# Two more Strassen pairs in the output projections of a transformer block, and a later place for one load

## The chip, the cores and the metric

One core of a Trainium2 chip runs the whole program. The metric is the device time of one execution in microseconds; lower is better.

## The reference

One block of a streaming encoder on 256 tokens of width 2048, in float32: a SwiGLU feed-forward layer, a mixer of two attentions (A: 16 heads of 64 with a clipped relative bias; B: latent attention, 16 heads), cross attention over 256 memory tokens (4 heads of 512), and a second feed-forward layer, each with a residual and a layer norm behind it. What matters here is the output side of the mixer and of the cross attention:

```python
y_b = mla_attention(...) @ w_o_b                 # 256x2048 @ 2048x2048
mix = (g_a * y_a + g_b * y_b) @ w_out
h = layer_norm(ALPHA * h + mix, ...)
m = layer_norm(mem, mem_ln_g, mem_ln_b)          # 256 memory tokens
kv = m @ w_xkv ; q = h @ w_xq
xa = softmax(q @ k.T / sqrt(512)) @ v @ w_xo     # 256x2048 @ 2048x2048
h = layer_norm(ALPHA * h + xa, ...)
```

## The kernel before

**Arithmetic.** Each float32 operand is split into a high part `hi` (a cast to fp32r on ScalarE, L264) and a rest `lo` (a subtraction on VectorE, L267). A product is three TensorE passes: hi·hi, lo(x)·hi(w), hi(x)·lo(w).

**Units.** A weight matrix comes in raw tiles of 128x2048 (1 MB) through SyncE's DMA queue into three buffers, in the order of use, up to two units ahead of TensorE. In a *pair group* (`pair_group`) a unit holds two K tiles of 128 rows for 1024 columns of output. Group g makes 1024 of the 2048 columns for all 256 tokens, so a unit updates four PSUM tiles of 128x512; a 2048-row matrix has eight units, c = 0 to 7.

**Plain and Strassen units.** A plain unit (`mm_pair`, L311) is 2 K tiles x 4 PSUM tiles x 3 passes = 24 matmuls of 512 columns. A unit that is listed in the group's `at` is taken as one 2x2 Strassen-Winograd step (`mm_sums`, L366): seven products, 21 matmuls. It needs four sums of the weight's quarters (`weight_sums`, L248 and L250, VectorE), `hi` and `lo` of three of the raw quarters and of the four sums, and four sums of the activation (`sum_forms`, L321 and L325, then a split, L255 and L256). The order of its products is: high part of raw quarters, low part of them, high part of the sums, low part of the sums. When the next unit is a Strassen unit too, the halves change places, so that the buffers of the sums come free early (`close`). Behind the group's last Strassen unit `shared` combines four extra PSUM tiles (L679 to L684).

**Homes.** The host stores a Strassen unit's weight quarters in another order, so `at` is also an argument of the layout. `sums_in` names the blocks of on-chip memory for hi, lo and the staging of the sums; a `SUMS_` table names for each unit c the block in which the activation's sums stay, or `None` for small pool buffers.

**The order of work.** The kernel's Python code lists items; `weave` puts side work in front of the i-th item of a group. A tile framework then schedules all instructions, so an engine's order follows the list only roughly. On the chip each engine takes its instructions in its own fixed order.

**The places that are touched.**
- `out_b(g)` in `mixer`: the two groups of `y_b @ w_o_b`. Group 0 has Strassen units 2, 4, 6 (`AT_YB[0]`), group 1 has 4 and 6. Behind each group `done` multiplies by the gates (L1282 to L1284) and copies 16-bit planes (L846) for DMA transposes (L850), which SyncE issues between weight loads; `turn` joins the planes again (L854) and splits them (L255, L256) into the operand `mix` of the next product, 512 columns at a time. Group 0's transposes run during group 1, and group 1's during the first units of `mix @ w_out`.
- `mem_norm`: loads the memory tokens (`mem`, into blocks T1 and T2) and the transposed memory (`memT`, into T3 and H4) from GpSimd's DMA queue at item 0 of the `w_out` product. Statistics follow at items 4 and 7, and the quarters of the normalised memory at items 10 to 14.
- `cross`: the first output group of `w_xo` (`out_pair` with `SUMS_XO`) has Strassen units 2, 4, 6 in natural order. Among its first units stand the last two heads' products, `out(2)` and `out(3)` (L1543), which use the same kind of PSUM tile (`mm`) as the group's four extra tiles.

Of the kernel before, what the change touches and what calls it, by code (L numbers as in the profile page):

```python
# [21 lines left out]
KT = D // P  # L22
# [10 lines left out]
ORDER_GATE = (0, 2, 1, 4, 5, 3, 6, 7)  # L33
SUMS_YB = {4: ("T0", 0), 6: ("T0", 1), 2: None}
AT_YB = (2, 4, 6), (4, 6)
SUMS_XQ = {4: ("H5", 0), 6: ("H5", 1), 2: None}
SUMS_XV = {4: ("T3", 0), 6: ("T3", 1), 2: None}
SUMS_XO = {2: None, 4: ("H2", 0), 6: ("H2", 1)}

AT_XQ = (4, 6), (2, 4, 6)  # L40
AT_XV = (2, 4, 6), (4, 6)
SUM_HOME = ("X2", "X3"),
# [59 lines left out]
class Kernel:  # L102
# [515 lines left out]

    def out_pair(self, bank, src, g, nk, x, at, fx, scale, st, sums_in=SUM_HOME):

        nc, h = self.nc, self.h
        ps, qs = {}, {}
# [10 lines left out]
        def finish():  # L633
            for tt in range(2):
                for a in range(2):
                    self.finish(tt, 2 * g + a, ps[tt, a], scale and not at, st)
        self.pair_group(bank, src, 512, nk, x, at, fx, ps, qs, shared, sums_in)
        self.add(finish)
# [692 lines left out]
    def mem_norm(self):  # L1331

        nc, t = self.nc, self.t
        e = self.mem = {}

        def load():
            e["m"] = [self.block(f"T{1 + tt}", (P, D)) for tt in range(2)]
            e["raw"] = [self.block(g) for g in ("T3", "H4")]
            for j in range(2):
                nc.gpsimd.dma_start(e["m"][j], t["mem"][j])  # L1340
            for j in range(2):
                nc.gpsimd.dma_start(e["raw"][j], t["memT"][:, 8 * j:8 * j + 8, :])
# [40 lines left out]

        return {0: [load], 4: [stat(0)], 7: [stat(1)], 9: [spread], 10: [quarter(0)], 11: [quarter(1)], 13: [quarter(2)], 14: [quarter(3)]}

# [47 lines left out]
    def cross(self, xT, st, norm, steps_out):  # L1433
        nc, t, e = self.nc, self.t, self.mem
        q, k, v, sc, pt, o, turned = {}, {}, {}, {}, {}, {}, {}
        fq, fv, fx = {}, {}, {}
        m, x = lambda: e["mT"], lambda: o["t"]
# [113 lines left out]
        form = lambda c: self.forms_step(fx, SUMS_XO, c, x)  # L1551
# [14 lines left out]
        scale, planes, nsend, njoin = norm  # L1566
# [13 lines left out]
        def all_items():  # L1580
            self.out_pair(1, t["w_xo"][0], 0, KT, x, SUMS_XO, fx, True, st, (("T0", "T1"), "T3"))
            self.out_proj("w_xo_r", KT, x, True, st, steps_out, (
                ("T0", "T1", "early"), ("T2", "T3", "early"), ("H0", "H1", "early"), ("H2", "H3", "early")), 2)
        self.weave(self.collect(all_items), {1: [out(2), out(3), form(2)], 2: [form(4)], 4: [form(6)]}, prio=0)

# [191 lines left out]
```

## Time and profile before

| | |
|---|---|
| timed runs | 2434.51, 2434.72, 2436.06 us; median 2434.72 us |
| the profiled execution's own time | 2432.88 us |
| its span | 2431.0 us |
| granted TensorE clock | 1.000 |
| ScalarE, GpSimd busy | 1553.1 us (64%), 36.0 us (1%) |
| HBM traffic | 200 GB/s over the span |

Matmuls are pipelined and their ends are modelled, so a TensorE busy for 100% is told apart from a waiting one only by the start times of successive matmuls. Stretches in what follows are us from the span's start: `out_b(0)` runs from 1200.14 to 1241.62, `out_b(1)` to 1283.78, the first group of `w_out` to 1327.59, and the first output group of the cross attention, with the two heads' products in it, from 1649.68 to 1697.34.

### The profile page before, as it was taken

The page shows a single profiled execution, that of the slowest core. Times are in us where ns is not written, and L with a number is a line of the kernel's source. Part 1 is how long each engine was busy: PE and PEld are TensorE (multiplying, and loading weights), DVE is VectorE, ACT ScalarE, POOL GpSimd, SP SyncE. Part 2 cuts the span into 40 slices and gives each one's busy share as a digit, 9 for nine tenths or more (in the row PEclk, how much of TensorE's full clock was granted, in tenths as well). Part 3 has the DMA queues.
Part 4 walks back from the last instruction along what each step waited for, and adds up shares of the span by engine and source line. Part 5 has one row for each costly group of instructions (what it writes and reads, how often), then busy time and mean ns, then how long its engine had stood idle before and what let it go on. Part 6 is the DMA issues. An engine that isn't in the chain of part 4 may idle for free.

```text
span 2431.0 us, 29704 instructions
## 1 busy us (share of the span) xinstructions
PE 2422.4 (100%) x11280; PEld 2021.5 (83%) x11280; DVE 2131.3 (88%) x2437; ACT 1553.1 (64%) x2022; POOL 36.0 (1%) x81
## 2 busy tenths in 40 slices
PE   9999999999999999999999999999999999999999
PEld 8888888889888888888888888888888888888887
DVE  8999989899889998789788889879879999888997
ACT  6676745666555557878565787755666675556662
POOL 0000000000000001000000000000000000000000
PEclk9999999999999999999999999999999999999999
DMA  7766656667645657776577577655556766666665
GB/s 267 253 211 215 206 201 223 210 202 230 218 174 211 216 202 242 236 203 176 186 254 246 170 237 214 216 183 192 191 199 213 228 222 211 219 207 207 201 222 180
DMA packets 176416, 516.21 MB, mean 212 GB/s; under 512 B 111729, under 2 KB 112497, under 8 KB 121105
## 3 DMA queue, kind: packets, MB, share of 16 engines
q1 hardware_dynamic: 170816, 495.83, 61.5%
q0 software_dynamic: 4592, 17.30, 2.3%
q8 instruction: 88, 1.44, 0.2%
q10 hardware_dynamic: 864, 1.18, 0.1%
q14 instruction: 56, 0.45, 0.1%
HBM read 485.30 MB, written 2.10 MB: 200 GB/s over the span
## 4 chain that ended last, share of the span: by engine, by line
PE 89%; DVE 4%; ACT 3%; DMA 2%; issue 1%; SPq 0%; DVEq 0%; ACTq 0%
PE at L311 25%; PE mm L311 24%; PE at L366 11%; PE mm L366 11%; PE mm L298 10%; PE mm L277 4%; PE mm L279 2%; DVE lo L267 2%; ACT hi L264 2%; PE at L1034 1%; DMA raw<-w_xq 1%; DMA raw<-w_xk 0%; DMA raw<-w_xv 0%; PE at L1088 0%; ACT w L832 0%
## 5 line engine op out<-in xcount | busy, mean ns | idle before, releaser
L264 ACT CAST hi<-raw 128x1024 fp32r<-128x1024 f32 (+1 forms) x852 | 803.4, 980 | 440.4 <-PE at L311 130.5
L267 DVE TENSOR_TENSOR lo<-raw,hi 128x2048 fp32r<-128x2048 f32 (+1 forms) x427 | 902.2, 2115 | 136.1 <-ACT hi L264 129.1
L311 PE MATMUL mm<-hi,T 128*128 128x512 f32 (+1 forms) x1312 | 308.1, 384 | 0.5 <-ACT hi L255 0.4
L264 ACT CAST X<-H 128x1024 fp32r<-128x1024 f32 (+1 forms) x170 | 174.7, 1034 | 171.5 <-DVE H L248 117.5
L311 PEld LDWEIGHTS mm<-hi,T 128*128 128x128 f32 x1312 | 244.4, 188 | 46.8 <-ACT hi L255 0.9
L311 PE MATMUL at<-hi,T 128*128 128x512 f32 x1136 | 272.3, 390 | 0.0
L311 PEld LDWEIGHTS at<-hi,T 128*128 128x128 f32 x1136 | 213.3, 188 | 44.4
L267 DVE TENSOR_TENSOR X<-H,X 128x2048 fp32r<-128x2048 f32 (+1 forms) x85 | 191.5, 2253 | 62.1 <-ACT X L264 61.9
L311 PE MATMUL mm<-lo,T 128*128 128x512 f32 (+1 forms) x656 | 158.1, 383 | 0.0
L311 PE MATMUL at<-lo,T 128*128 128x512 f32 x568 | 141.0, 390 | 0.0
L311 PEld LDWEIGHTS mm<-lo,T 128*128 128x128 f32 x656 | 122.2, 188 | 22.4
L311 PE MATMUL at<-hi,H 128*128 128x512 f32 x560 | 133.4, 390 | 0.0
L311 PEld LDWEIGHTS at<-lo,T 128*128 128x128 f32 x568 | 106.7, 188 | 22.1
L311 PEld LDWEIGHTS at<-hi,H 128*128 128x128 f32 x560 | 105.0, 188 | 21.5
L250 DVE TENSOR_TENSOR H<-H,raw 128x512 f32<-128x512 f32 (+1 forms) x170 | 115.7, 681 | 2.4
L311 PE MATMUL mm<-hi,H 128*128 128x512 f32 x480 | 115.6, 392 | 0.4 <-DVE w L684 0.4
L311 PEld LDWEIGHTS mm<-hi,H 128*128 128x128 f32 x480 | 89.6, 188 | 19.5 <-DVE w L684 0.8
L248 DVE TENSOR_TENSOR H<-raw 128x1024 f32<-128x1024 f32 (+1 forms) x85 | 102.2, 1203 | 0.5 <-DMA raw<-w_gate 0.3
L366 PE MATMUL mm<-X,X 128*128 128x512 f32 x342 | 91.3, 392 | 0.0
L264 ACT CAST X<-raw 128x1024 fp32r<-128x1024 f32 (+1 forms) x54 | 55.4, 1035 | 48.7 <-DVE raw L250 38.7
L366 PE MATMUL at<-X,X 128*128 128x512 f32 (+1 forms) x315 | 82.7, 386 | 0.0
L854 ACT COPY w<-w 128x1024 uint16<-128x1024 uint16 (+1 forms) x60 | 75.6, 1273 | 1.5 <-DMA w<-w 1.4
(387 smaller groups left out, 4153.9 us busy)
## 6 DMA issues: line engine op xcount, KB each, us to landing
raw<-ffn_w_in SPq DMA_DIRECT2D x150, 1024.0 KB, 4.9
raw<-ffn_w_out SPq DMA_DIRECT2D x66, 1024.0 KB, 4.9
raw<-w_gate SPq DMA_DIRECT2D x32, 1024.0 KB, 4.7
raw<-ffn_w_out_r SPq DMA_DIRECT2D x16, 1024.0 KB, 5.0
raw<-w_qk SPq DMA_DIRECT2D x16, 1024.0 KB, 5.3
raw<-w_o_b SPq DMA_DIRECT2D x16, 1024.0 KB, 4.8
raw<-w_out SPq DMA_DIRECT2D x16, 1024.0 KB, 5.1
raw<-w_xk SPq DMA_DIRECT2D x16, 1024.0 KB, 5.3
```

Of the source, the lines that this page charges most:

```text
L248: self.nc.vector.tensor_tensor(two[0], two[1], raw[:, :m].unsqueeze(1).to_broadcast([P, 2, m]), ALU.add)
L250: self.nc.vector.tensor_tensor(t[:, a * m:a * m + m], t[:, b * m:b * m + m], raw[:, a * m:a * m + m], ALU.add)
L264: self.last_hi = self.nc.scalar.copy(hi[:, c:d], src[:, c:d])
L267: self.last_lo = self.nc.vector.tensor_tensor(lo[:, :n], src, hi[:, :n].bitcast(F32), ALU.subtract)
L277: self.nc.tensor.matmul(ps, hi[j], x.both(kt), start=(j == 0), stop=False)
L279: self.last_mm = self.nc.tensor.matmul(ps[:, :S], lo[j], x.at(0, kt), start=False, stop=(j == n - 1))
L298: self.last_mm = self.nc.tensor.matmul(ps, x.at(xi, kt)[:, tt * P:(tt + 1) * P], w[wi][:, j * 512 + c:j * 512 + c + m], start=(start and j ...
L311: self.last_mm = self.nc.tensor.matmul(ps[tt, g][:, :n], x.at(xi, kt)[:, tt * P:(tt + 1) * P], w[wi][:, c:c + n], start=first and j + wi + ...
L366: self.last_mm = self.nc.tensor.matmul(bank[:, :m], a[xi], v[wi][:, c * m:(c + 1) * m], start=own and first and wi + xi == 0, stop=own and ...
L854: self.nc.scalar.copy(self.words(u, n).rearrange("p (c k) -> p k c", k=2), self.words(s, n).rearrange("p (k c) -> p k c", k=2))
L1034: nc.tensor.matmul(ps[:, c0:c0 + nk], q[:, tt * P:(tt + 1) * P], k[:, :nk], start=(j == 0), stop=(j == len(parts) - 1))
```

## The change

It has three parts. **(1)** `out_b(1)` takes units 2, 4 and 6 as Strassen units instead of 4 and 6; the activation's sums for unit 2, which group 0 uses already, move from pool buffers to block F, so that they last through both groups. **(2)** The first output group of `w_xo` takes units 0, 2, 4 and 6 as Strassen units, and its units run in the order 1, 0, 3, 2, 4, 5, 6, 7; the sums for unit 0 are formed in front of the group's first item and live in block F. **(3)** In `mem_norm` the two loads of the transposed memory move from item 0 to item 5.

```diff
-SUMS_YB = {4: ("T0", 0), 6: ("T0", 1), 2: None}
-AT_YB = (2, 4, 6), (4, 6)
+SUMS_YB = {4: ("T0", 0), 6: ("T0", 1), 2: ("F", 0)}
+AT_YB = (2, 4, 6), (2, 4, 6)
-SUMS_XO = {2: None, 4: ("H2", 0), 6: ("H2", 1)}
+SUMS_XO, ORDER_XO = {2: None, 4: ("H2", 0), 6: ("H2", 1), 0: ("F", 0)}, (1, 0, 3, 2, 4, 5, 6, 7)
...
-    def out_pair(self, bank, src, g, nk, x, at, fx, scale, st, sums_in=SUM_HOME):
+    def out_pair(self, bank, src, g, nk, x, at, fx, scale, st, sums_in=SUM_HOME, order=None):
...
-        self.pair_group(bank, src, 512, nk, x, at, fx, ps, qs, shared, sums_in)
+        self.pair_group(bank, src, 512, nk, x, at, fx, ps, qs, shared, sums_in, order)
...
         def load():
             e["m"] = [self.block(f"T{1 + tt}", (P, D)) for tt in range(2)]
-            e["raw"] = [self.block(g) for g in ("T3", "H4")]
             for j in range(2):
                 nc.gpsimd.dma_start(e["m"][j], t["mem"][j])
+
+        def load_turned():
+            e["raw"] = [self.block(g) for g in ("T3", "H4")]
             for j in range(2):
                 nc.gpsimd.dma_start(e["raw"][j], t["memT"][:, 8 * j:8 * j + 8, :])
...
-        return {0: [load], 4: [stat(0)], 7: [stat(1)], 9: [spread], 10: [quarter(0)], 11: [quarter(1)], 13: [quarter(2)], 14: [quarter(3)]}
+        return {0: [load], 4: [stat(0)], 5: [load_turned], 7: [stat(1)], 9: [spread], 10: [quarter(0)], 11: [quarter(1)], 13: [quarter(2)], 14: [quarter(3)]}
...
-            self.out_pair(1, t["w_xo"][0], 0, KT, x, SUMS_XO, fx, True, st, (("T0", "T1"), "T3"))
+            self.out_pair(1, t["w_xo"][0], 0, KT, x, SUMS_XO, fx, True, st, (("T0", "T1"), "T3"), ORDER_XO)
...
-        self.weave(self.collect(all_items), {1: [out(2), out(3), form(2)], 2: [form(4)], 4: [form(6)]}, prio=0)
+        self.weave(self.collect(all_items), {0: [form(0)], 1: [out(2), out(3), form(2)], 2: [form(4)], 4: [form(6)]}, prio=0)
```

The scheduled order changes with it. ScalarE at the start of `out_b(1)`, before; H0 and H1 are the gate blocks of group 0 whose planes go to the transposes (L846), and the `raw` tiles 1574, 1581, 1584, 1587 are units 1, 2, 3, 4:

```order
L264 CAST hi_1575_9961<-raw_1574_9959 128x1024 x2
L264 CAST hi_1582_10010<-raw_1581_10008 128x1024
L846 COPY H0_885_5874<-H0_885_5874 128x1024 x2
L264 CAST hi_1582_10010<-raw_1581_10008 128x1024
L264 CAST hi_1585_10041<-raw_1584_10039 128x1024 x2
L846 COPY H1_933_6171<-H1_933_6171 128x1024 x2
L264 CAST hi_1589_10078<-raw_1587_10046 128x1024
L264 CAST hi_1589_10078<-raw_1587_10046 128x512
```

The same place after the change; raw 1571, 1574, 1584, 1587 are units 1, 2, 3, 4, X3 holds the weight sums of unit 2 and H5 their high part:

```order
L264 CAST hi_1572_9952<-raw_1571_9950 128x1024 x2
L264 CAST H5_1582_10010<-X3_1575_9959 128x1024
L264 CAST hi_1580_10005<-raw_1574_9957 128x1024
L846 COPY H0_885_5874<-H0_885_5874 128x1024 x2
L264 CAST hi_1580_10005<-raw_1574_9957 128x512
L264 CAST hi_1585_10041<-raw_1584_10039 128x1024
L846 COPY H1_933_6171<-H1_933_6171 128x1024 x2
L264 CAST H5_1582_10010<-X3_1575_9959 128x1024
L264 CAST hi_1585_10041<-raw_1584_10039 128x1024
L264 CAST hi_1593_10079<-raw_1587_10046 128x1024
```

Unit 2's raw quarters are cast in two instructions (1024 and 512 columns), its sums in two more. The second cast of the sums (the second H5 row) stands behind the two plane copies of H1.

ScalarE in the first output group of the cross attention, before; X2 and X3 become the operands of the output product for heads 2 and 3, T3 and T0 hold a Strassen unit's weight sums and their high part, here those of unit 2, and w1 the activation's sums for it:

```order
L255 CAST X2_2065_13374<-mm_2067_13384 128x256
L255 CAST X2_2065_13374<-mm_2068_13393 128x256
L264 CAST T0_2063_13369<-T3_2054_13318 128x1024
L255 CAST X2_2065_13374<-mm_2069_13402 128x256
L264 CAST T0_2063_13369<-T3_2054_13318 128x1024
L255 CAST X3_2070_13411<-mm_2071_13412 128x256
L255 CAST X3_2070_13411<-mm_2072_13421 128x256
L255 CAST X3_2070_13411<-mm_2073_13430 128x256
L255 CAST X3_2070_13411<-mm_2074_13439 128x256
L264 CAST hi_2082_13493<-raw_2081_13491 128x1024 x2
L255 CAST w1_2075_13448<-w2_2080_13453 128x128
```

And after; T3 and T0 belong to unit 0 here, and F holds its activation's sums:

```order
L255 CAST X2_2070_13387<-mm_2072_13397 128x256
L255 CAST X2_2070_13387<-mm_2073_13406 128x256
L255 CAST X2_2070_13387<-mm_2074_13415 128x256
L264 CAST T0_2054_13317<-T3_2047_13271 128x1024
L255 CAST F_2058_13336<-w2_2060_13338 128x512
L255 CAST X3_2075_13424<-mm_2076_13425 128x256
L255 CAST X3_2075_13424<-mm_2077_13434 128x256
L255 CAST X3_2075_13424<-mm_2078_13443 128x256
L255 CAST X3_2075_13424<-mm_2079_13452 128x256
L264 CAST hi_2090_13505<-raw_2068_13381 128x1024
L255 CAST w1_2080_13461<-w2_2085_13466 128x128
```

The cast into F, one row behind unit 0's second T0 cast, now stands in front of the four casts of head 3 (X3).

TensorE at the same place, before; H4 and H5 are the operands for heads 0 and 1, hi_2051 and lo_2052 the plain unit 1, and the products of head 3 write mm tiles from X1 and X0:

```order
L311 MATMUL at_2057_13336<-hi_2051_13311,H4_1973_12758 128x512 x2
L1543 MATMUL mm_2071_13412<-X1_2039_13209,X0_2056_13329 128x256 x6
L311 MATMUL at_2058_13337<-hi_2051_13311,H4_1973_12758 128x512 x2
L1543 MATMUL mm_2072_13421<-X1_2039_13209,X0_2056_13329 128x256 x6
L1543 MATMUL mm_2073_13430<-X1_2039_13209,X0_2056_13329 128x256 x6
L1543 MATMUL mm_2074_13439<-X1_2039_13209,X0_2056_13329 128x256 x6
L311 MATMUL at_2059_13338<-hi_2051_13311,H4_1973_12758 128x512 x2
L311 MATMUL at_2060_13339<-hi_2051_13311,H4_1973_12758 128x512 x2
L311 MATMUL at_2057_13336<-lo_2052_13312,H4_1973_12758 128x512
```

And after; T0 and T1 are the high and low part of unit 0's weight sums, hi_2066 and lo_2067 the plain unit 3, and hi_2052 raw quarters of unit 0:

```order
L366 MATMUL at_2063_13348<-T0_2054_13317,H4_1973_12755 128x512 x2
L311 MATMUL at_2061_13346<-hi_2066_13376,H5_2000_12936 128x512 x2
L311 MATMUL at_2064_13349<-hi_2066_13376,H5_2000_12936 128x512 x2
L311 MATMUL at_2061_13346<-lo_2067_13377,H5_2000_12936 128x512
L311 MATMUL at_2064_13349<-lo_2067_13377,H5_2000_12936 128x512
L311 MATMUL at_2061_13346<-lo_2067_13377,H5_2000_12936 128x512
L311 MATMUL at_2064_13349<-lo_2067_13377,H5_2000_12936 128x512
L366 MATMUL at_2063_13348<-T1_2055_13318,H4_1973_12755 128x512
L311 MATMUL at_2063_13348<-hi_2066_13376,H5_2000_12936 128x512 x4
L311 MATMUL at_2063_13348<-lo_2067_13377,H5_2000_12936 128x512 x2
L366 MATMUL at_2062_13347<-hi_2052_13312,F_2058_13336 128x512
L1545 MATMUL mm_2076_13425<-X1_2039_13206,X0_2057_13329 128x256 x6
```

Head 3's products now stand behind the first product with T1 and the first with F.

GpSimd's queue with the memory loads, before; the row ahead of them clears a constant tile that `stat(0)` uses:

```order
L1349 MEMSET w1_1643_10438 128x128
L1340 DMA T2_1622_10291<-mem 128x2048
L1342 DMA T3_1623_10292<-memT 128x2048
L1342 DMA H4_1624_10293<-memT 128x2048
L1340 DMA T1_1621_10290<-mem 128x2048
```

And after:

```order
L1351 MEMSET w1_1641_10431 128x128
L1339 DMA T2_1622_10288<-mem 128x2048
L1344 DMA T3_1651_10486<-memT 128x2048
L1344 DMA H4_1652_10487<-memT 128x2048
L1339 DMA T1_1621_10287<-mem 128x2048
```

The four loads stand in the same order behind the same row: `mem` into T2, `memT` into T3 and H4, `mem` into T1.

## The prediction

> **What bounds the kernel now.** The page's first part and its summary of the chain of waits come first.
>
> ```profile
> PE 2422.4 (100%) x11280; PEld 2021.5 (83%) x11280; DVE 2131.3 (88%) x2437; ACT 1553.1 (64%) x2022; POOL 36.0 (1%) x81
> PE 89%; DVE 4%; ACT 3%; DMA 2%; issue 1%; SPq 0%; DVEq 0%; ACTq 0%
> ```
>
> TensorE (PE) is the bound, and VectorE (DVE) is close behind at 88%. How close it is in the touched places is read from the windows, one for each output group: length, then busy time and count of instructions by engine. The first two are untouched groups of the feed-forward layer for comparison, with four Strassen units each; then come `out_b(1)`, the first group of `w_out`, and the output group of the cross attention.
>
> ```profile
> core 0: us, PE busy (x) PEld busy (x) DVE busy (x) ACT busy (x) POOL busy (x), PEclk, DMA share, GB/s
> 729.03:769.83 40.80, 40.80 (x181) 33.81 (x181) 35.86 (x30) 23.24 (x28) 0.00 (x0) 1.00 0.63 222
> 769.83:811.49 41.66, 41.63 (x181) 33.58 (x181) 38.30 (x30) 25.06 (x28) 0.53 (x1) 1.00 0.57 198
> 1241.62:1283.78 42.16, 42.16 (x188) 34.93 (x186) 38.28 (x35) 30.44 (x35) 1.60 (x3) 1.00 0.82 276
> 1283.78:1327.59 43.81, 43.81 (x194) 35.97 (x193) 34.63 (x43) 26.78 (x29) 0.53 (x1) 1.00 0.79 252
> 1649.68:1697.34 47.66, 47.66 (x233) 39.87 (x232) 47.16 (x64) 28.78 (x43) 0.00 (x0) 1.00 0.54 186
> ```
>
> The clock is 1.00 throughout. VectorE fills 38.28 of 42.16 us in `out_b(1)` (91%) and 47.16 of 47.66 us (99%) in the cross output group: there it is as much the bound as TensorE.
>
> The price of a matmul comes from the timeline of TensorE, from start to start.
>
> ```profile
> 1649.68 3.79 PE L311 MATMUL at<-hi,H 128*128 128x512 f32 x16
> 1653.31 1.98 PE L311 MATMUL at<-lo,H 128*128 128x512 f32 x8
> 1655.12 3.04 PE L1543 MATMUL mm<-X,T 128*128 128x256 f32 x24
> 1657.99 2.46 PE L311 MATMUL at<-hi,H 128*128 128x512 f32 x10
> ```
>
> A plain unit, 24 matmuls, takes 1655.12 - 1649.68 = 5.44 us, or 0.2267 us each, and the next starts with no gap. A Strassen unit's 21 take 4.76 us. A head's 24 narrow products take 2.87 us.
>
> **What the two pairs remove and add.** Each pair removes three matmuls: 2 x 3 x 0.2267 = **1.36 us** on TensorE. What a Strassen unit asks of VectorE is seen just there, in the rows of unit 2.
>
> ```profile
> 1653.63 2.29 DVE L267 TENSOR_TENSOR lo<-raw,hi 128x2048 fp32r<-128x2048 f32 x1
> ...
> 1656.44 1.23 DVE L248 TENSOR_TENSOR T<-raw 128x1024 f32<-128x1024 f32 x1
> 1657.57 1.76 DVE L267 TENSOR_TENSOR lo<-raw,hi 128x1536 fp32r<-128x1536 f32 x1
> 1659.24 0.69 DVE L250 TENSOR_TENSOR T<-T,raw 128x512 f32<-128x512 f32 x1
> ...
> 1660.17 0.69 DVE L250 TENSOR_TENSOR T<-T,raw 128x512 f32<-128x512 f32 x1
> ...
> 1661.98 2.29 DVE L267 TENSOR_TENSOR T<-T,T 128x2048 fp32r<-128x2048 f32 x1
> ```
>
> A plain unit needs the first row alone, 2.29. A Strassen unit needs 1.23 + 2 x 0.69 for the weight's sums, 1.76 for the raw quarters' low part and 2.29 for the sums': 6.66, that is **4.37 us more**. The cross output also forms the activation's sums for unit 0.
>
> ```profile
> 1672.27 0.70 DVE L321 TENSOR_TENSOR w<-X 128x512 f32<-128x512 f32 x1
> 1673.00 0.50 DVE L325 TENSOR_TENSOR w<-w 128x128 f32<-128x128 f32 x2
> 1673.41 0.29 DVE L325 TENSOR_TENSOR w<-w,w 128x128 f32<-128x128 f32 x1
> ...
> 1675.69 0.28 DVE L325 TENSOR_TENSOR w<-w,w 128x128 f32<-128x128 f32 x1
> 1675.92 2.29 DVE L267 TENSOR_TENSOR T<-T,T 128x2048 fp32r<-128x2048 f32 x1
> 1678.12 0.68 DVE L256 TENSOR_TENSOR H<-w,H 128x512 fp32r<-128x512 f32 x1
> ```
>
> That is 0.70 + 0.50 + 0.29 + 0.28 + 0.68 = 2.45, so 6.8 us of VectorE go into the cross output group, and 4.4 into `out_b(1)`, where the activation's sums exist already. ScalarE gets some 1.5 us of casts a unit. SyncE's weight loads stay: a stored unit has the same bytes.
>
> **Term 1, `out_b(1)`.** These are the rows of TensorE (units 2, 3, 4 and 5 start at 1252.50, 1257.94, 1263.38 and 1268.14), of VectorE and of ScalarE.
>
> ```profile
> 1252.50 3.79 PE L311 MATMUL at<-hi,T 128*128 128x512 f32 x16
> 1257.94 3.79 PE L311 MATMUL at<-hi,T 128*128 128x512 f32 x16
> 1263.38 0.61 PE L366 MATMUL at<-hi,H 128*128 128x512 f32 x2
> 1268.14 3.79 PE L311 MATMUL at<-hi,H 128*128 128x512 f32 x16
> 1251.58 1.22 DVE L1284 TENSOR_TENSOR H<-H 128x1024 f32<-128x1024 f32 x1
> 1264.44 1.23 DVE L248 TENSOR_TENSOR X<-raw 128x1024 f32<-128x1024 f32 x1 [2.27 <-DMA raw<-w_o_b]
> 1252.84 2.00 ACT L846 COPY H<-H 128x1024 uint16<-128x1024 uint16 x2
> 1261.93 2.00 ACT L264 CAST hi<-raw 128x1024 fp32r<-128x1024 f32 x2 [2.09 <-DMA raw<-w_o_b]
> 1263.84 2.58 ACT L854 COPY H<-H 128x1024 uint16<-128x1024 uint16 x2
> ```
>
> An engine takes its rows in order, so the new order decides. (a) The second cast of unit 2's sums stands behind the two H1 copies, which wait for L1284, ready at about 1251.9: copies to 1253.9, cast (half of 2.00) to 1254.9, VectorE's low part (2.29, and a hand-over) to 1257.3. TensorE asks for that part after 17 of 21 matmuls, at 1252.50 + 3.85 = 1256.35: a wait of **1.0**. (b) The same cast of unit 4 stands behind both casts of unit 5's weights, which land at 1261.93, and behind one L854 copy: 1261.9 + 1.9 + 1.3 + 1.05 + 2.3 = 1268.5, half a microsecond more if the load comes as late as (a) makes it, say 1268.75. Unit 4 starts at 1263.38 - 0.68 + 1.0 = 1263.7 and asks at 1267.55: a wait of **1.2**. (c) For unit 6 the casts of unit 7 stand in front, whose buffer comes free some 3.8 us into unit 5: 3.8 + 1.9 + 2.2 + 2.3 = 10.2, against 5.44 + 3.85 = 9.3: **0.9**. So 3.1 of waits less 0.68 saved, **+2.4**. If nothing stood badly, VectorE's 42.16 - 38.28 = 3.9 idle and its lead would hide the 4.4, and the term is -0.7; if the casts come twice as late as needed, 6.2 - 0.7 = +5.5.
>
> I take +2.4: no row before shows a ScalarE instruction passing another that stands ahead of it.
>
> The Trainium skill, "TensorE: Matmul & The Clock Gate", section "Architectural detail: the array is 16× 32×32, not 1× 128×128", says that only TensorE may take a weight load ahead of its turn and that ScalarE and VectorE work strictly in order. By it this term would be +2.4; if a ready cast could pass a waiting copy it would be -0.7. The rows of before agree with it.
>
> **Term 2, the first group of `w_out`.** VectorE comes out of `out_b(1)` later by up to 4.4 - 2.4 = 2.0 us against TensorE, and group 1's planes and transposes with it. TensorE starves a little there already:
>
> ```profile
> 1305.54 4.08 PE L311 MATMUL mm<-hi,T 128*128 128x512 f32 x16
> ```
>
> Sixteen such matmuls took 3.79 elsewhere, so 0.29 is lost. VectorE's 34.63 of 43.81 us speaks for full recovery, so the term lies between 0 and 2.0; I take **+0.8**. Its upper end does not go with term 1's, as both are paid from the same 4.4.
>
> **Term 3, the cross output.** I follow VectorE from the last row that is alike and look at where it had a lead.
>
> ```profile
> 1647.52 0.68 DVE L682 TENSOR_TENSOR w<-w,w 128x512 f32<-128x512 f32 x1
> 1689.15 4.49 DVE L267 TENSOR_TENSOR lo<-raw,hi 128x2048 fp32r<-128x2048 f32 x2
> 1691.90 3.79 PE L311 MATMUL at<-hi,X 128*128 128x512 f32 x16
> ```
>
> In the new order there follow, up to the end of the sums that the cast into F needs: two L248 (1.13 each, start to start above), thirteen operations of 512 columns (0.60 each), 1.67, two of 2.20, and four L325 (0.9): 17.1, so from 1648.1 to 1665.2; the cast of 512 columns (about 0.6, half of a 1024-column one) makes 1665.8. The low part of the sums, before it in that list, is ready at about 1663.2. TensorE does unit 1 to 1655.12, head 2 to 1658.0, then 17 matmuls of units 0 and 3 to 1661.9, where it asks for that low part: it waits 1.4. Seven more end at 1664.9; the next reads F: 1.0. Meanwhile VectorE has another 29.5 us from 1665.2 to unit 6's sums' low part (six L250, two L248, three of 1.67, four of 2.20, three each of L321 and of splits at 0.6, eight narrow at 0.33, sixteen 128-column ones at 0.22): 1694.7, or 1695.8 if it waits about a microsecond for ScalarE. Behind that part stand 23 matmuls, 5.2 us: the group ends at 1699.9 to 1701.1 instead of 1697.34, the saving counted. I take **+3.4**. As a check from throughput: unit 7's low part was ready at 1691.4 and asked for at 1691.90 + 3.63 = 1695.5, a lead of 4.1; 6.8 less this lead and less the 0.5 idle gives +2.2 at least. If VectorE waits a little more, +4.0.
>
> **Term 4, the memory load.** In the profile before, GpSimd (POOL) issues it here.
>
> ```profile
> 1264.09 0.54 POOL L1342 DMA_DIRECT2D T<-memT  x1 [10.59 <-ACT hi L264]
> 1274.04 0.53 POOL L1342 DMA_DIRECT2D H<-memT  x1 [9.41 <-PE at L311]
> 1289.63 2.62 SPq L850 DMA_TRANSPOSE H<-H  x2
> ```
>
> Both are issued ahead of these transposes (SP's queue), released when blocks come free. After the change the queue of GpSimd shows the same four loads in the same order, so the part moves nothing: **0**. If it did, it could win about the 0.29 of step 4.
>
> **Sum.** +2.4 + 0.8 + 3.4 + 0 = **+6.6 us**, on the profiled execution's 2432.88 us 2439.5. That execution was 1.84 us below the median of the timed runs, 2434.72; for that median I predict **2441.3 us**.
>
> **Rivals.** *Throughput alone decides.* Orders that stand badly cost nothing because the waits fall into gaps that I do not see; then `out_b(1)` gives -0.7, `w_out` 0 and the cross output +2.2: **+1.5**, 2436.2. For it: the second window has four Strassen units with VectorE at 92% (38.30 of 41.66) and is 0.86 us over the first; nothing like 3.1. Against it: the plane copies and joins that stand in ScalarE's way are absent there (25.06 busy against 30.44).
>
> *All cover holds.* The first window shows four Strassen units in 40.80 us, exactly 180 x 0.2267, with VectorE at 35.86. If VectorE in the cross output can take its 6.8 us in the attention's stretch before 1649.68, where form(0) is listed first, only the saving is left: **-1.36**, 2433.4. It needs VectorE to enter the group 4.6 us (6.8 less 2.2) or more further ahead than now; from that point on the change is not slower. Against it: the order puts those operations behind L682.
>
> *The load does what its name says*, with at most 0.3 us; term 4 speaks against it.
>
> **Chances.** Forecast 0.55, throughput 0.30, all cover 0.10, and 0.05 for something above. A difference of 0.2% (4.9 us) is about what a measurement can tell from none. The forecast's own span is +3 to +9.5 (5.5 and 4.0), a fifth of it below 4.9: same 0.11 + 0.28 + 0.06 = 0.45; faster 0.04, which would take more than the saving alone; slower 0.51. The range runs from the all-cover time, 2433.4, to 2434.72 + 9.5 and the 1.3 by which a timed run stood above the median: 2445.5.
>
> **What would show it.** In the windows after: `out_b(1)` near 44.6 us and the cross output near 51, with gaps in TensorE's starts ahead of the products with the low part of sums (units 2, 4, 6; in the cross output unit 0's, then F's), put down to VectorE's L267 behind ScalarE's casts. An `out_b(1)` of 41.5 fells term 1, a cross output below 49 term 3. GpSimd's loads of `memT` issued behind the transposes would fell term 4.

## The result and the profile after

| | before | after |
|---|---|---|
| timed runs, median | 2434.23 us (7 runs, 2433.15 to 2436.06) | 2441.72 us (7 runs, 2439.31 to 2448.86) |
| ratio after to before | | 1.0039, 95% interval 1.003 to 1.0048 |
| the profiled execution's own time | 2432.88 us | 2439.31 us |
| span | 2431.0 us | 2437.5 us |

The change makes the kernel slower by 0.39%; 2441.3 us was predicted. The timed runs also spread more: 9.6 us from lowest to highest against 2.9, and the profiled execution of after is the fastest of its seven.

These are lines of the profile page of after, busy time by engine and the summary of the chain of waits:

```profile
PE 2425.1 (99%) x11274; PEld 2017.9 (83%) x11274; DVE 2139.9 (88%) x2448; ACT 1556.0 (64%) x2024; POOL 35.9 (1%) x81
PE 83%; DVE 7%; ACT 4%; DMA 3%; issue 2%; SPq 0%; DVEq 0%; ACTq 0%
```

The six matmuls are gone. TensorE's share of the chain fell from 89% to 83%, and VectorE's rose from 4% to 7%. The windows show where; the columns are those of the windows before, and the rows are `out_b(0)`, `out_b(1)`, the first group of `w_out` and the cross output group:

```profile
1200.46:1241.94 41.48, 41.48 (x185) 34.35 (x183) 34.37 (x27) 21.71 (x25) 0.00 (x0) 1.00 0.60 215
1241.94:1284.98 43.04, 42.30 (x185) 34.01 (x183) 38.96 (x35) 32.16 (x37) 1.59 (x3) 1.00 0.79 271
1284.98:1329.96 44.98, 44.44 (x194) 35.73 (x192) 36.56 (x46) 26.64 (x29) 0.53 (x1) 1.00 0.77 245
1651.23:1701.98 50.75, 48.41 (x229) 38.58 (x228) 50.36 (x71) 30.64 (x45) 0.00 (x0) 1.00 0.43 153
```

`out_b(1)` went from 42.16 to 43.04, the first `w_out` group from 43.81 to 44.98, the cross output from 47.66 to 50.75: +0.88, +1.17, +3.09. The stretch behind the cross output, up to the matmul that started at 1759.91 before, is 1.06 us longer too (63.63 against 62.57). What is left of the 6.5 us between the two spans is small differences of both signs: +0.32 ahead of `out_b(0)`, -0.83 between `w_out`'s first group and the cross output, +0.82 behind it all.

The lost time stands as gaps in TensorE's starts. This is its timeline of after; a bracket gives the idle time and who ended it. Start to start the waits are a little longer than the bracket: the seven matmuls at 1277.57 should end with a next start at 1277.57 + 7 x 0.2267 = 1279.16, and it came at 1280.06, so 0.90.

```profile
1256.67 0.84 PE L311 MATMUL at<-hi,T 128*128 128x512 f32 x3
1257.48 0.98 PE L366 MATMUL mm<-X,F 128*128 128x512 f32 x3
...
1277.57 1.75 PE L311 MATMUL at<-hi,T 128*128 128x512 f32 x7
1280.06 0.97 PE L366 MATMUL mm<-X,T 128*128 128x512 f32 x3 [0.74 <-DVE X L267]
...
1286.89 2.34 PE L311 MATMUL mm<-hi,X 128*128 128x512 f32 x9 [0.16 <-DVE w L684]
...
1307.79 4.20 PE L311 MATMUL mm<-hi,T 128*128 128x512 f32 x16 [0.38 <-ACT T L255]
...
1664.58 0.50 PE L366 MATMUL at<-T,H 128*128 128x512 f32 x1 [0.90 <-DVE T L267]
1667.18 0.50 PE L366 MATMUL at<-hi,F 128*128 128x512 f32 x1 [0.69 <-ACT F L255]
1692.00 0.73 PE L311 MATMUL at<-hi,X 128*128 128x512 f32 x2 [0.53 <-ACT hi L264]
1692.95 0.73 PE L366 MATMUL at<-T,X 128*128 128x512 f32 x2 [0.22 <-ACT T L264]
```

In `out_b(1)` one large wait stands in front of unit 6's low part of the sums. The two waits at the head of the cross output (1.06 and 0.86 start to start) are on the sums' low part and on the cast into F, and two shorter ones come near its end.

### The profile page after: what moved, and what is told of

Same layout as the page of the kernel before. It is cut to its first block, busy times and chain, and to the rows that moved or that the text cites. A ratio compares the mean times of both kernels' runs of the same rounds, so it can differ in the third digit from the quotient of the medians.

```text
span 2437.5 us, 29705 instructions
## 1 busy us (share of the span) xinstructions
PE 2425.1 (99%) x11274; PEld 2017.9 (83%) x11274; DVE 2139.9 (88%) x2448; ACT 1556.0 (64%) x2024; POOL 35.9 (1%) x81
## 4 chain that ended last, share of the span: by engine, by line
PE 83%; DVE 7%; ACT 4%; DMA 3%; issue 2%; SPq 0%; DVEq 0%; ACTq 0%
PE at L311 23%; PE mm L311 22%; PE at L366 10%; PE mm L366 10%; PE mm L298 9%; PE mm L277 4%; DVE lo L267 2%; ACT hi L264 2%; PE mm L279 2%; PE at L1034 1%; DMA raw<-w_xq 1%; DMA raw<-w_xv 0%; ACT H L854 0%; DVE raw L250 0%; PE at L277 0%
## 5 line engine op out<-in xcount | busy, mean ns | idle before, releaser
L250 DVE TENSOR_TENSOR H<-H,raw 128x512 f32<-128x512 f32 (+1 forms) x170 | 115.3, 678 | 2.4
L248 DVE TENSOR_TENSOR H<-raw 128x1024 f32<-128x1024 f32 (+1 forms) x85 | 102.0, 1200 | 0.6 <-DMA raw<-w_gate 0.3
```

Source lines behind the costliest of these rows:

```text
L248: self.nc.vector.tensor_tensor(two[0], two[1], raw[:, :m].unsqueeze(1).to_broadcast([P, 2, m]), ALU.add)
L250: self.nc.vector.tensor_tensor(t[:, a * m:a * m + m], t[:, b * m:b * m + m], raw[:, a * m:a * m + m], ALU.add)
```

## The experiments

Besides the page, one number of each run is used throughout: the length of a stage, taken between the starts of the same matmuls as above. `out_b(1)` and the first `w_out` group are given together as well, since a wait can move from one to the other. A median is to be read by its distance from that of before in the last column, as before itself moved by up to 1.3 us between these series: after lies 7.5 us above it.

| run | `out_b(1)` | first `w_out` group | both | cross output | median, us | runs of before beside it |
|---|---|---|---|---|---|---|
| before | 42.16 | 43.81 | 85.97 | 47.66 | 2434.23 | |
| after | 43.04 | 44.98 | 88.02 | 50.75 | 2441.72 | 2434.23 |
| part 1 alone | 43.21 | 45.01 | 88.22 | 47.57 | 2439.23 | 2433.52 |
| part 2 alone | 42.16 | 43.80 | 85.96 | 50.84 | 2437.78 | 2433.52 |
| part 3 alone | 42.16 | 43.84 | 86.00 | 47.54 | 2433.18 | 2433.52 |
| after, unit 0 late | 49.16 | 44.97 | 94.13 | 54.03 | 2444.85 | 2433.52 |
| after, F's sums on GpSimd | 42.83 | 45.04 | 87.87 | 49.25 | 2438.27 | 2433.21 |
| after, H1's transposes later | 41.93 | 45.48 | 87.41 | 50.89 | 2440.97 | 2433.21 |
| after, no `memT` loads | 41.82 | 45.56 | 87.38 | 50.65 | 2438.81 | 2433.21 |
| after, first `memT` load moved | 42.07 | 44.89 | 86.96 | 50.57 | 2439.12 | 2433.21 |
| after, sums ahead of the next unit | 41.48 | 49.78 | 91.26 | 50.75 | 2445.05 | 2432.92 |
| part 1, sums ahead of the next unit | 41.48 | 48.71 | 90.19 | 47.54 | 2438.27 | 2432.92 |

### The parts alone

Part 1, the kernel before with only this:

```diff
-SUMS_YB = {4: ("T0", 0), 6: ("T0", 1), 2: None}
-AT_YB = (2, 4, 6), (4, 6)
+SUMS_YB = {4: ("T0", 0), 6: ("T0", 1), 2: ("F", 0)}
+AT_YB = (2, 4, 6), (2, 4, 6)
```

> Part 1 alone: the third pair in the second group of w_o_b, the rest as before. In the trace of the changed kernel that group is 0.88 us longer than before and the first group of w_out 1.2 us longer. If these stages pay for their own pair (static order of ScalarE and VectorE), this kernel is 2 us slower than before (1.5 to 2.6), with a wait of about 0.9 us in front of unit 6's low part of the sums and about 1 us in the first group of w_out. Rival: VectorE's idle time hides it and the loss in the changed kernel came from the moved load; then this one is 0.7 us faster than before. The timed runs of the changed kernel spread over 9.5 us; if this part is the cause of the spread, these runs spread by as much, if not, by the 3 us of before.

Measured: ratio 1.0021 (1.0012 to 1.003). The profiled execution took 2434.66 us, 1.8 over before's, with the two stages 2.25 us longer and the waits as expected (0.95 at unit 6, then 0.46 and 0.94 us in `w_out`). But the eleven timed runs fall into two groups: five from 2434.66 to 2435.96, six from 2439.23 to 2443.32. The median is 5.7 us above that of before, where 1.5 to 2.6 was expected. Against the same median this part costs 1 to 2.5 us in one group and 6 to 10 in the other, and the spread of the changed kernel is largely of this part.

Part 2, the kernel before with `SUMS_XO`, `ORDER_XO` and `form(0)` alone:

```diff
-SUMS_XO = {2: None, 4: ("H2", 0), 6: ("H2", 1)}
+SUMS_XO, ORDER_XO = {2: None, 4: ("H2", 0), 6: ("H2", 1), 0: ("F", 0)}, (1, 0, 3, 2, 4, 5, 6, 7)
...
+        self.weave(self.collect(all_items), {0: [form(0)], 1: [out(2), out(3), form(2)], 2: [form(4)], 4: [form(6)]}, prio=0)
```

> Part 2 alone: the fourth pair in the cross output with its order of units, the rest as before. By the order theory 3.1 us slower than before (2.2 to 4.0): the window of the group 50.7 us instead of 47.66, with waits near 1.1 us on the sums' low part and 0.9 us on the cast into F. If part of the 3.1 us came from VectorE entering the group late because of the earlier stages, less than 2.2. Rival: VectorE finds the 6.8 us in the attention's stretch and it is faster by 0.7.

Measured: ratio 1.0019 (1.001 to 1.0028), the group 50.84 us, with the same four waits as in after (1.13, 0.86, 0.67, 0.39 start to start). The loss of 3.2 us in the group is part 2's own and owes nothing to the earlier stages; the stretch behind it is 1.1 us longer here too (63.67). With that the median, 4.3 us above before's, is a little over the range expected.

This profile is of the slowest of the eleven runs, 2440.9 us, and 2.99 us of it were lost ahead of `out_b(1)`, which began at 1244.61 instead of 1241.62. The longest wait there, 2.15 us in front of the matmul at 681.62, stands in a stage that no part touches, and the profile shows nothing that it waited for. In the fourteen profiles `out_b(1)` begins between 1241.28 and 1242.02 in eight and between 1242.62 and 1244.61 in six. So some of what sets runs apart lies outside the touched stages; its cause was not tried. The lengths of the touched stages leave it out, the medians do not.

Part 3, the kernel before with `load_turned` at item 5 alone:

```diff
+        def load_turned():
+            e["raw"] = [self.block(g) for g in ("T3", "H4")]
...
+        return {0: [load], 4: [stat(0)], 5: [load_turned], 7: [stat(1)], 9: [spread], 10: [quarter(0)], 11: [quarter(1)], 13: [quarter(2)], 14: [quarter(3)]}
```

> Part 3 alone: the transposed memory loaded at item 5, the rest as before. The order theory says nothing moves: GpSimd issues the four loads at the same times within 0.5 us, and the time is that of before within 0.5 us. Rival: the later place in the list lets the scheduler put other work ahead of it and the first group of w_out gains its 0.2 us of waits, or the runs begin to spread as those of the changed kernel do.

Measured: ratio 1.0001 (0.9992 to 1.001), runs from 2431.82 to 2434.84. GpSimd's queue issues the loads where it did (1264.09 and 1274.04 before):

```profile
1263.75 0.53 POOL L1344 DMA_DIRECT2D T<-memT  x1 [10.59 <-ACT hi L264]
1273.70 0.53 POOL L1344 DMA_DIRECT2D H<-memT  x1 [9.42 <-PE at L311]
```

Part 1 alone was run twice more, for the profile of a run of the upper group:

> Part 1 alone once more, for one profile: six of its eleven timed runs took 2439 us and more, five 2436 us and less, and the profile in hand is of the second kind. In a run of the first kind the second w_o_b group shows the wait on unit 6's sums at 3 to 4 us instead of 0.95, behind a load of unit 7 that lands 5 us later, as the profile of the kernel with unit 0 late does. If the group takes 43.2 us in a slow run too, the spread comes from elsewhere.

> The same once more, for a second profile: each run is of the slow kind with a chance of about one half.

Both were of the lower group: 2434.84 and 2435.04 us, `out_b(1)` 42.47 and 42.69, waits of 0.57 and 0.73 at unit 6. A profile of part 1 itself in the upper group was not caught.

### The cross output: load of VectorE, or place in its queue?

Unit 0 late:

```diff
-SUMS_XO, ORDER_XO = {2: None, 4: ("H2", 0), 6: ("H2", 1), 0: ("F", 0)}, (1, 0, 3, 2, 4, 5, 6, 7)
+SUMS_XO, ORDER_XO = {2: None, 4: ("H2", 0), 6: ("H2", 1), 0: ("F", 0)}, (1, 3, 2, 5, 4, 6, 0, 7)
...
-        self.weave(self.collect(all_items), {0: [form(0)], 1: [out(2), out(3), form(2)], 2: [form(4)], 4: [form(6)]}, prio=0)
+        self.weave(self.collect(all_items), {1: [out(2), out(3), form(2)], 2: [form(4)], 4: [form(6)], 5: [form(0)]}, prio=0)
```

> The changed kernel with unit 0 of the cross output late: order 1, 3, 2, 5, 4, 6, 0, 7 and its activation's sums formed at item 5. The work of VectorE is the same, but nothing reads F early. If VectorE's throughput sets the cost of the fourth pair, the two waits near the group's start go, and the time returns as a wait near the end: the group stays within 0.7 us of the changed kernel's 50.75 us. If the place of F's forms and of the sums in the order sets it, the two waits of 1.06 and 0.86 us are won, and the group takes 48.8 us; the program is then 1.9 us faster than the changed kernel.

Measured: ratio 1.0046 (1.0034 to 1.0059); the group took 54.03 us. The two early waits went, and others, of up to 1.64 us, came in the group's second half. That waits come back speaks for the first theory, but neither range held: the group is 5.2 us over the 48.8 of the second theory, and 2.6 us over even the upper end of the first:

```profile
1696.93 0.50 PE L366 MATMUL at<-T,X 128*128 128x512 f32 x1 [1.47 <-DVE T L267]
1697.79 1.01 PE L366 MATMUL mm<-T,H 128*128 128x512 f32 x3 [0.35 <-ACT H L255]
1698.60 0.63 PE L366 MATMUL at<-hi,H 128*128 128x512 f32 x1
1699.03 2.77 PE L366 MATMUL mm<-T,H 128*128 128x512 f32 x6
```

Part of the excess is pace: the six matmuls from 1699.03 to 1701.60 take 0.43 us each instead of 0.2267, 1.2 us together. The rest is not explained. This kernel's `out_b(1)`, which this edit doesn't touch, took 49.16 us; that is read below.

F's five sums on GpSimd (`eng`, VectorE for all other sums):

```diff
-        nc.vector.tensor_tensor(v, x.blk(0, k, 2).bitcast(F32), x.blk(1, k, 2).bitcast(F32), ALU.add)
+        eng.tensor_tensor(v, x.blk(0, k, 2).bitcast(F32), x.blk(1, k, 2).bitcast(F32), ALU.add)
...
-            nc.vector.tensor_tensor(f[:, j], a, b, op)
+            eng.tensor_tensor(f[:, j], a, b, op)
...
-        self.weave(self.collect(all_items), {0: [form(0)], 1: [out(2), out(3), form(2)], 2: [form(4)], 4: [form(6)]}, prio=0)
+        self.weave(self.collect(all_items), {0: [self.forms_step(fx, SUMS_XO, 0, x, eng=nc.gpsimd)], 1: [out(2), out(3), form(2)], 2: [form(4)], 4: [form(6)]}, prio=0)
```

> The changed kernel with the five sums for unit 0 of the cross output (one row of 512 columns, four of 128) on GpSimd instead of VectorE; their split stays. VectorE loses 1.77 us of work in front of F. If VectorE's load sets this group's length, the wait of 0.86 us on the cast into F goes and the window falls from 50.75 by 1 to 1.8 us, to about 49.3. Rival: GpSimd is slower at these sums than VectorE by more than it saves, F comes later still, and the window is as long or longer.

Measured: ratio 1.0026 (1.0016 to 1.0036). These are GpSimd's timeline, TensorE's only long wait in the group (1.56 us from start to start), and the group's window; most line numbers are one higher here:

```profile
1644.09 2.11 POOL L326 TENSOR_TENSOR w<-w 128x128 f32<-128x128 f32 x2 [4.69 <-ACT T L855]
1646.17 1.00 POOL L326 TENSOR_TENSOR w<-w,w 128x128 f32<-128x128 f32 x2
```

```profile
1681.99 0.73 PE L367 MATMUL at<-T,X 128*128 128x512 f32 x2 [1.40 <-ACT T L264]
```

```profile
1652.11:1701.36 49.25, 47.85 (x229) 38.79 (x228) 48.52 (x64) 30.39 (x45) 0.00 (x0) 1.00 0.44 154
```

GpSimd had the sums done by 1647.2, five microseconds ahead of the group; both waits at its head went, a new one came in its middle, and 1.77 us less on VectorE made the group 1.50 us shorter. VectorE still fills 48.52 of 49.25 us. This edit takes load off VectorE and makes F early at once. But the wait on F was only 0.86 us, and with unit 0 late, where nothing reads F early and the load stays, nothing was won. Together the two runs say that VectorE's load sets the group's length, and the place of F's forms only where the wait shows; that it does so nearly one for one rests on this one step of 1.77 us.

### `out_b(1)`: a late load, or the place behind it?

First what the wait at unit 6 hangs on in after: ScalarE's and then VectorE's timeline.

```profile
1273.48 2.00 ACT L264 CAST hi<-raw 128x1024 fp32r<-128x1024 f32 x2 [1.04 <-DMA raw<-w_o_b]
1275.38 1.05 ACT L264 CAST H<-X 128x1024 fp32r<-128x1024 f32 x1
```

```profile
1275.51 2.29 DVE L267 TENSOR_TENSOR lo<-raw,hi 128x2048 fp32r<-128x2048 f32 x1 [1.80 <-ACT hi L264]
1277.72 2.28 DVE L267 TENSOR_TENSOR X<-X,H 128x2048 fp32r<-128x2048 f32 x1
```

Both engines take unit 7 first: ScalarE waits for its weights to land, casts them, and only then makes the second cast of unit 6's sums; VectorE forms unit 7's low part ahead of that of the sums, for which TensorE waits. Unit 7's load was issued at 1265.36 and landed at 1273.40, 8.0 us later. In the kernel before it took 7.6 us too (1264.66 to 1272.24) and TensorE did not wait, for there both engines take unit 6's sums first; again ScalarE's and then VectorE's timeline:

```profile
1268.25 2.03 ACT L264 CAST H<-X 128x1024 fp32r<-128x1024 f32 x2
...
1273.66 2.00 ACT L264 CAST hi<-raw 128x1024 fp32r<-128x1024 f32 x2
```

```profile
1271.38 2.29 DVE L267 TENSOR_TENSOR X<-X,H 128x2048 fp32r<-128x2048 f32 x1
...
1275.69 2.29 DVE L267 TENSOR_TENSOR lo<-raw,hi 128x2048 fp32r<-128x2048 f32 x1 [0.82 <-ACT hi L264]
```

In the run with unit 0 late (the same `out_b(1)`) it was issued at 1270.50 and landed at 1279.82, and the same places read:

```profile
1279.90 1.99 ACT L264 CAST hi<-raw 128x1024 fp32r<-128x1024 f32 x2 [4.35 <-DMA raw<-w_o_b]
1281.79 1.04 ACT L264 CAST H<-X 128x1024 fp32r<-128x1024 f32 x1
```

```profile
1282.89 1.22 PE L366 MATMUL mm<-H,T 128*128 128x512 f32 x2 [3.55 <-ACT H L264]
```

```profile
1282.89:1290.00 7.11, 7.11 (x19) 5.60 (x20) 5.51 (x6) 6.35 (x8) 0.00 (x0) 0.57 0.82 334
```

One wait of 3.71 us, and behind it a granted clock of 0.57 over 7.1 us: 6.1 us more than in after. A run of part 1 in which the load is late by some microseconds would be longer by about what its upper group shows; no profile of such a run shows that it is so. Five runs take the wait apart.

The transposes of H1 behind unit 7's load:

```diff
-            return {2: [send(0)], 4: [send(1)], 5: [turn(0)], 6: [turn(1)]}
+            return {2: [send(0)], 5: [turn(0)], 6: [send(1)], 7: [turn(1)]}
```

> The changed kernel with the second transposes of the first w_o_b group (H1) sent two items later, behind the load of unit 7's weights, and joined one item later. In the changed kernel unit 7's load was issued at 1265.36 and landed at 1273.40, beside those transposes and the first memT load. If the wait in front of unit 6's low part of the sums comes from the late landing (casts of unit 7 ahead of the second cast of unit 6's sums), the load lands about 2 us earlier, the wait of 0.9 us goes, the second w_o_b group takes 42.1 us or less, and the timed runs spread by 3 us like before instead of 9.5; the median falls by 2 to 4 us. Rival: the order on VectorE alone makes the wait; then it stays.

Measured: ratio 1.0036 (1.0024 to 1.0048). The load, issued at 1264.96, landed in 4.9 us instead of 8.0, and `out_b(1)` has no wait above 0.13 us left (41.93 us). But it was now also issued 0.16 us ahead of the first `memT` load (1265.12), where in after it came 1.33 us behind it, so this run does not tell the transposes from the memory load. The joins of H1 now delay VectorE's L684, which frees the PSUM tile for `w_out`:

```profile
1287.63 2.56 PE L311 MATMUL mm<-hi,X 128*128 128x512 f32 x10 [1.12 <-DVE w L684]
```

Of 1.11 us won, 0.50 were given back at once. The median did not fall by 2 to 4 us: it lies 7.8 us above that of before beside it, where after lies 7.5 above. The runs still spread by 10 us, with one of six at 2448.64.

Without the loads of the transposed memory:

```diff
-                nc.gpsimd.dma_start(e["raw"][j], t["memT"][:, 8 * j:8 * j + 8, :])
+                nc.gpsimd.memset(e["raw"][j], 1.0)
```

> The changed kernel without the two loads of the transposed memory: the blocks are filled with ones on GpSimd instead (2 MB less traffic, the attention over the memory gets other data). If the memory load beside the weights and the transposes is what makes unit 7's weights late, the wait on unit 6's sums goes and the spread with it: the median falls by 2 to 4 us. If the transposes alone make them late, nothing changes by more than 0.5 us in the profile, and the spread stays.

Measured: ratio 1.0026 (1.0014 to 1.0038). Unit 7's load took 5.0 us (1266.77 to 1271.77), the wait went (41.82), and 0.58 of the 1.22 us came back in `w_out` as a longer wait at 1308.38. The median lies 5.6 us above before's, 1.9 us less than after does, a little under the 2 to 4 expected; the spread did not go, and of ten runs one was at 2451.57.

The third part made real, with a copy ahead of the first load that waits for the transposes' output (`self.mark` is the last block that `send` transposes):

```diff
+                if j == 0:
+                    nc.gpsimd.tensor_copy(e["raw"][0].bitcast(U16).rearrange("p a b -> p (a b)")[:, :2], self.mark[:, :2])
                 nc.gpsimd.dma_start(e["raw"][j], t["memT"][:, 8 * j:8 * j + 8, :])
```

> The changed kernel with the move that the third part names made real: the first memT load waits on GpSimd for the last DMA transposes of the mix (a copy of two elements from their output into the block it loads). Both loads then start after about 1305 us instead of 1264 and 1274. If the memory load's place costs the changed kernel its late weights, this gains what the kernel without these loads gains (2 to 4 us of median), less what the later loads cost in the w_out groups. By my prediction's term 4 it gains 0.3 us at most. A loss of over 1 us would mean that the normalised memory is late for its first use.

Measured: ratio 1.0027 (1.0016 to 1.0037). Only one of the two loads moved, as GpSimd's queue shows; the other went ahead of the copy:

```profile
1275.92 0.53 POOL L1347 DMA_DIRECT2D H<-memT  x1 [20.44 <-PE at L311]
...
1305.90 1.86 POOL L1346 COPY T<-H 128x2 uint16<-128x2 uint16 x1 [19.23 <-DMA H<-H]
1308.05 0.53 POOL L1347 DMA_DIRECT2D T<-memT  x1 [0.30 <-POOL T L1346]
```

That is the load which stood beside unit 7's in after (1264.03). Unit 7's took 5.2 us, the wait at unit 6 went, the two stages took 86.96 us, the best of all kernels with the third pair, and the seven runs lie between 2437.78 and 2441.37, their median 5.9 us above before's. Over all fourteen profiles unit 7's load goes with this one: in eleven the first `memT` load was issued 0.6 to 4.5 us ahead of it, and it took 7.15 to 9.3 us; in the other three that load was issued behind it, moved away or left out, and it took 4.9 to 5.2. So the memory load's place matters once the third pair stands there; the third part of the change, as written, doesn't reach it.

Last, the loads left as they are and the order changed: a plain unit of the `w_o_b` groups behind the sums ahead of it.

```diff
+                if i and isinstance(queue[i - 1], Sums) and queue[i - 1].tags == ("H5", "X2"):
+                    first = self.last_hi
+                    self.behind_lo = self.last_lo
...
-        with self.tc.issue_after(self.chain.ins) if self.chain is not None else nullcontext():
+        chain, self.behind_lo = getattr(self, "behind_lo", None) or self.chain, None
+        with self.tc.issue_after(chain.ins) if chain is not None else nullcontext():
```

> The changed kernel with one rule of order more: in the w_o_b groups a plain unit's casts and its low part come behind the casts and the low part of the Strassen unit's sums ahead of it. No work is added or removed. ScalarE then has both casts of unit 6's sums ahead of unit 7's casts. If the place in ScalarE's and VectorE's queues is the cause, the wait of 0.9 us (and of 4 us where the load is late) in front of unit 6's sums goes though the loads stay where they are: the second w_o_b group takes 41.5 to 41.8 us instead of 43.04, the slow runs of part 1 (2439 us and more, against 2435) grow rare, and the median falls by 2 to 4 us. Rival: the late load is the cause by itself; then TensorE waits as long one step later, for unit 7's high part, and neither the group nor the spread changes.

> Part 1 alone with the same rule of order. If order was all that the third pair cost, this is 0.7 us faster than before, at best the same as before within what can be measured, and its runs spread by 3 us. What stays of the loss in the first w_out group (1.2 us) would show as 0.5 us slower than before.

Measured: ratios 1.0053 (1.0041 to 1.0065) and 1.0027 (1.0017 to 1.0037). In both, `out_b(1)` takes 41.48 us, that is 183 x 0.2267: not one wait, with unit 7's load landing 7.15 us after its issue. In the first of the two, ScalarE makes the second cast of unit 6's sums ahead of unit 7's casts, as it does before the change:

```profile
1273.33 1.05 ACT L267 CAST H<-X 128x1024 fp32r<-128x1024 f32 x1 [1.37 <-DVE X L253]
1274.29 1.05 ACT L267 CAST hi<-raw 128x1024 fp32r<-128x1024 f32 x1
```

The place behind unit 7 is what turned the late load into a wait. But the same rule moved other work: VectorE now does `out_b(1)`'s gating (L1286 to L1288 here) ahead of the low part of `w_out`'s first weights, and TensorE waits for that; in after the low part began at 1283.35 and the gating at 1286.75. The timelines of VectorE and TensorE, and the windows, of the first of the two:

```profile
1288.06 2.28 DVE L271 TENSOR_TENSOR lo<-raw,hi 128x2048 fp32r<-128x2048 f32 x1
```

```profile
1290.40 3.78 PE L315 MATMUL mm<-lo,X 128*128 128x512 f32 x8 [3.47 <-DVE lo L271]
```

```profile
1283.14:1332.93 49.79, 46.32 (x194) 37.74 (x193) 36.85 (x44) 27.84 (x30) 0.53 (x1) 0.93 0.72 222
1290.40:1295.68 5.28, 5.28 (x12) 4.12 (x13) 5.28 (x4) 3.35 (x4) 0.00 (x0) 0.50 1.00 302
```

The medians lie 12.1 us above before's for the whole change (7.5 without the rule) and 5.4 for part 1 (5.7 without it), and the runs spread by 11 us in both. No kernel with a part of the change beat the one before; it stays the fastest but for part 3 alone, which is not told apart from it.

## Why the prediction was right, and where its steps were off

**The sum.** For the profiled execution 2439.5 us was worked out and 2439.31 measured. That closeness is luck: the terms came to +0.9, +1.2 and +3.1 where +2.4, +0.8 and +3.4 stood, 5.1 together, and the 1.3 up to the measured 6.4 are made up by 1.06 us behind the cross output and small differences, which no term had.

**Term 1 (+2.4, measured +0.88)** had the right mechanism in the wrong size, and of its three waits only one came. The times at which VectorE has the sums' low part were good: 1257.3 worked out for unit 2 and 1257.4 measured (1255.13 + 2.29), 1268.5 to 1269.0 for unit 4 and 1268.5 measured. (For unit 2 the working took L1284 as ready at 1251.9 without showing from what; by its own row it ends at 1252.80 in before, and in after it ended at 1251.71.) The step that failed is "TensorE asks for that part after 17 of 21 matmuls": the new order of TensorE, which the working left out for this stage, puts 3, 6 and 7 matmuls of the next unit's high part in front of it. They cover 0.7, 1.4 and 1.6 us, so (a) came to 0.24, (b) to 0.04, and only (c) is left with 0.90. There the cover was used up because ScalarE waited 1.04 us for unit 7's load, which the working had not counted. The mechanism, a place behind unit 7 in ScalarE's and VectorE's queue, is shown by the order runs: the wait goes with the place alone, and `out_b(1)` comes out 0.68 us shorter than before, the -0.7 that the working gives if nothing stands badly.

**Term 2 (+0.8, measured +1.17)** was somewhat low. Part 1 alone has it too (+1.20), part 2 alone has none (43.80): it is the third pair's. The mechanism was as written: VectorE began the gating 0.26 us ahead of the `w_out` group before (1283.52) and 1.77 us into it after (1286.75), 2.0 us later against TensorE, and the transposes were issued 7.25 us into the group instead of 5.85. Of the waits in the group, 0.94 us is on the operand that the transposes bring (from 1307.79) and 0.43 on L684 (1286.89), which the term did not name. Its size does not hang on the wait at unit 6: in the three runs that lose it by a change of loads or transposes the `w_out` group stayed at 44.9 to 45.6. The two stages together were never below 86.96, against 85.97 before, although TensorE has 0.68 us less to do.

**Term 3 (+3.4, measured +3.1)** went as written at its head: waits of 1.4 and 1.0 foretold, 1.06 and 0.86 measured, on the engines named. The late ones were put on VectorE's low part of unit 6's sums; they came earlier, on ScalarE's casts of unit 7's weights (1692.00) and of unit 6's sums (1692.95), which stand behind a cast that waited 3.87 us for VectorE's L248:

```profile
1689.95 1.05 ACT L264 CAST T<-T 128x1024 fp32r<-128x1024 f32 x1 [3.87 <-DVE T L248]
```

The low part itself was ready at 1696.35 (1694.06 + 2.29), 45.1 us behind the group's start, where 45.0 to 46.1 were worked out, and TensorE came to it only at 1696.77. That the load of VectorE is behind it rests on the runs with GpSimd and with unit 0 late, read together. What the term lacked is the 1.06 us behind the group (1743.65 and 1748.43 in after, at the next layer norm); part 2 alone shows it and part 1 doesn't, its cause was not tried.

**Term 4 (0)** held: part 3 alone is 1.0001. My "0.3 us at most" if the load did move was too low: moved in the changed kernel, one load gave 1.06 us in the two stages (one profile each; the three profiles of part 1 spread over 0.75), because it had been sharing the time of unit 7's weights, which I had not counted among its neighbours.

**The rule weighed against term 1**, that ScalarE and VectorE work strictly in order (the Trainium skill, "TensorE: Matmul & The Clock Gate", section "Architectural detail: the array is 16× 32×32, not 1× 128×128"), agrees with the queue shown above: unit 6's second cast, whose input was there at 1273.7 (L250), started at 1275.38 behind two casts that waited 1.04 us for a DMA.

**The rivals.** Throughput alone gave +1.5; its price for the cross output (+2.2) was too low by 0.9. All cover: no run supports it for the cross output, where VectorE entered the group as it did before. For the median, +7.5 came out where +6.6 stood, and there the closeness is luck too, for no step has a spread: six of the thirteen runs of part 1 are longer than the others by 4 to 8 us. That the late load makes them so is argued from one profile (the run with unit 0 late); a run of part 1 alone in the upper group was not seen in a profile, in kernels with that wait removed single runs near 2450 remain, and of 23 runs of the kernel before in one series one took 2440.28. The cause of the spread stays open.

## What to carry to other kernels

Saved matmuls are worth their time only where the engine that prepares the operands has room in that very window; in the cross output, with VectorE at 99%, 0.68 us saved on TensorE cost 6.8 us of sums on VectorE and 3 us of time. To place a wait, read the order of the engine that waits as closely as that of the one it waits for: the matmuls that a scheduler puts in between are the cover. And an item's place in the code's list is not its time of issue: look at the queue's rows before crediting a move, and at what shares the DMA engines there before calling it free.

## What was not expected of the hardware

In these traces a long wait of TensorE cost more than its length. Behind the waits of 3.63 us (both order runs) and 3.71 us (unit 0 late) the granted clock read 0.50 to 0.57, and matmuls started every 0.43 us instead of 0.2267 for 3 to 6 us, 1.7 to 3.0 us on top. In the cross output of the run with unit 0 late it came behind a cluster of four shorter waits, 0.55 to 1.64 us within 5 us. Single waits of up to 2.75 us (1746.97 in the run with the later transposes) had none of it, only about 0.1 us on a matmul that follows. And GpSimd's 128x128 sums took 0.5 to 1.05 us each where VectorE's took 0.2 to 0.3.
